# A hybrid attention layer: the products of the softmax weights with the values, for two tiles of keys at a time or for up to four

## The chip, the cores and the metric

The program runs on one core of a Trainium2 chip. The metric is the time of one execution on the device in microseconds (us); the figure for a kernel is the median of several executions.

## What is computed

One layer of a decoder with 1024 tokens and a width of 1024. Two mixers run in parallel on the same input: a gated delta rule over 8 heads, and sparse attention with 16 query heads in 4 groups of keys and values, 64 wide. After them come two gated projections and an MLP of width 4096. All is float32. The change touches the sparse attention alone, and of its three branches (compressed, selected, window) the second and third:

```
# selected: each query takes 8 blocks of 64 keys; window: each query takes the last 256 keys
s = q . k - slope * dist
p = softmax(where(mask, s, NEG))
o_slc, o_win = p_slc @ v_slc, p_win @ v_win
o = gate0 * o_cmp + gate1 * o_slc + gate2 * o_win
...
mix = sigmoid(g_dn) * (o_dn @ w_proj_dn) + sigmoid(g_ns) * (o @ w_proj_nsa)
x = x + mix @ w_out
x = x + relu(rmsnorm(x) @ w_up)^2 @ w_down
```

## The kernel before

The program has three stages. First come the projections of the input and the delta rule, then the sparse attention (about 1117 to 1589 us of the profiled span), then the output projections and the MLP.

The sparse attention is a list of 32 items: 4 groups (g) by 8 tiles of 128 queries (t). `item` (line 1113) plans one item i. Each piece of work is given a due time in units of items by `at3`; the pieces of all items are sorted by due time and written in that order (line 1369). The build then makes from it the order of the instructions of each engine, in which a piece may still be split or moved by a few places.

An item works on two branches. The selected branch (br 0) has t + 1 tiles of 128 keys, the window branch (br 1) up to three. For a tile of keys there are two pieces:

- `weights` (line 1242): TensorE writes the scores of four heads into a PSUM tile T of 128x512, by two matmuls with 512 columns (a third one, T<-cb, adds the causal mask on some tiles). ScalarE (ACT) takes the exponential into a tile P in SBUF. There are two banks for T and six buffers for P.
- `values` (line 1256): eight small products, one for each of four heads and two halves of the queries, with 64 columns of P as the stationary operand and 65 columns of the values as the moving one, summed into the PSUM tile O (in the trace o<-vv,P). O is one tile in one bank, used by all branches and items. In the order of the program such a product is one row, in the trace it is two matmuls: a tile of keys is 8 rows of the order and 16 matmuls of the trace.

After the last tile of a branch `join` (line 1264) reads O on VectorE (DVE): a reciprocal into coef, a product with the gate, a product into bs; POOL then adds bs to acc (VectorE does in the last item). After the window branch `turn_out` (line 1274) transposes acc on TensorE into a PSUM tile m, which has two banks, and `turn_store` stores it by ACT and a DMA.

Between these pieces TensorE also does the work of later items: `peak` (line 1210), scores into S (two banks) whose minimum VectorE takes; the compressed branch (tiles m); and `dn_part` (line 1336), the output projection of the delta rule, in g.

The change is in the due times of `values`. Tile j of n in an item is weighed at i + j/n. Its products are due at

```
lag = min(0.3, 2.5 / n)
j0 = j - (0 if br == 0 else t + 1)
e = i + (j + (j0 % 2 == 0 and not last)) / n + lag
```

where j0 counts the tiles within the branch: the products of an even tile are put to the time of the odd one behind it, so that they come in pairs.

Of the kernel before, what the change touches and what calls it, by code (L numbers as in the profile page):

```python
# [146 lines left out]
def body(ctx: ExitStack, tc: tile.TileContext, A, out):  # L147
# [825 lines left out]
    for h in range(NDN):  # L973
        head(h, s)
        last = s
# [117 lines left out]
    def at3(when, fn, *args):  # L1093
        if when < 0:
            when = max(1.6 * when, 1e-3 * when - 4.9)
        at(FULL + 1 + when, 0.5, fn, *args)
# [16 lines left out]
    def item(i, g, t):  # L1113
# [185 lines left out]
        for br in range(2):  # L1299
            n = spans[br][1]  # L1300
# [9 lines left out]
        n = len(tiles)  # L1310
        lag = min(0.3, 2.5 / n)
        for j, (br, k) in enumerate(tiles):
            at3(i + j / n, weights, br, k)
            first = j == 0 or tiles[j - 1][0] != br
            last = j == n - 1 or tiles[j + 1][0] != br

            j0 = j - (0 if br == 0 else t + 1)
            e = i + (j + (j0 % 2 == 0 and not last)) / n + lag
            times.append(e)
            at3(e, values, br, k, first, last)  # L1320
            if last:
                ends.append((e, join, turn_out, turn_store, br))
# [31 lines left out]
    for half in range(2):  # L1354
        at3(0.2 + 16 * half, dn_rows, half)
        for c in range(8):
            e = 1.5 + 2 * (8 * half + c)
            if half and c >= 6:
                e = 22 + 2 * c
# [5 lines left out]
    for i, (g, t) in enumerate(seq):  # L1365
        item(i, g, t)
# [382 lines left out]
```

## Time and profile before

| what | us |
|---|---|
| median of 3 runs | 2424.12 (2423.66 to 2424.78) |
| the profiled execution | 2423.24 |
| its span, first to last instruction | 2421.5 |
| TensorE (PE) busy | 2355.4 (97%) |
| VectorE (DVE) busy | 1565.8 (65%) |
| ScalarE (ACT) busy | 1092.0 (45%) |
| POOL busy | 565.7 (23%) |

PE is the time of matmuls, PEld that of the loads of their stationary operand, which can run beside matmuls. Matmuls overlap: one of 512 columns is listed with some 0.39 us, and the next starts 0.23 us after it. So the pace of TensorE is read from the starts in a timeline, not from the durations. A matmul is named by what it writes and reads, o<-vv,P for instance.

### The profile page before, as it was taken

How to read it: one execution, taken by the hardware profiler on the slowest of the kernel's cores; microseconds unless marked ns; L12 is line 12 of the kernel's file. 1: busy time of each engine (PE TensorE's matmuls, PEld its weight loads, DVE VectorE, ACT ScalarE, POOL GpSimd, SP SyncE). 2: the span in 40 equal slices, each digit the busy share in tenths (PEclk: the TensorE clock that was granted, in tenths of full speed). 3: DMA queues.
4: the chain of work that ended last, by engine and by line, in shares of the span. 5: the costliest groups of instructions: out<-in, count | busy, mean ns of one | idle time of the engine just before them, and what ended most of it. 6: DMA issues, size and time to landing. Idle time of an engine off the chain costs nothing. (4 is left out here: it accounts for less than half of the span.)

```text
span 2421.5 us, 44385 instructions
## 1 busy us (share of the span) xinstructions
PE 2355.4 (97%) x16673; PEld 1921.2 (79%) x16673; DVE 1565.8 (65%) x3626; ACT 1092.0 (45%) x2258; POOL 565.7 (23%) x473
## 2 busy tenths in 40 slices
PE   7999999999999999999999999999989999989999
PEld 5887878787878887876777777778877888878887
DVE  6666664747484848247777786643397666686785
ACT  4244343333343443227665766532256555534443
POOL 3132321203231423000010101012144444260320
PEclk9999999999999999999999999999999999999999
DMA  5421313131222221237442422164425443566343
GB/s 178 131 61 60 85 42 93 41 90 45 80 50 80 55 72 50 85 121 187 115 116 70 115 88 63 41 203 159 159 75 179 152 144 129 197 237 229 113 123 104
DMA packets 237510, 267.37 MB, mean 110 GB/s; under 512 B 76976, under 2 KB 128496, under 8 KB 237168
## 3 DMA queue, kind: packets, MB, share of 16 engines
q1 hardware_dynamic: 237296, 264.55, 35.6%
q8 instruction: 131, 2.15, 0.4%
q14 instruction: 83, 0.68, 0.1%
HBM read 190.05 MB, written 72.38 MB: 108 GB/s over the span
## 5 line engine op out<-in xcount | busy, mean ns | idle before, releaser
L177 PE MATMUL g<-hh,wh 128*128 128x512 f32 (+1 forms) x816 | 336.9, 413 | 6.7 <-ACT hh L174 6.0
L177 PE MATMUL g<-hl,wh 128*128 128x512 f32 (+1 forms) x816 | 328.6, 403 | 0.1
L177 PE MATMUL g<-hh,wl 128*128 128x512 f32 (+1 forms) x816 | 324.7, 398 | 0.1
L177 PE MATMUL V<-big,wh 128*128 128x512 f32 x768 | 238.2, 390 | 2.5 <-DVE c L1592 2.5
L186 DVE TENSOR_TENSOR wl<-a,wh 128x512 fp32r<-128x512 f32 x192 | 163.8, 855 | 111.3 <-ACT wh L174 111.3
L174 ACT ACTIVATE wh<-wr 128x512 fp32r<-128x512 f32 x210 | 131.9, 629 | 209.2 <-PE g L177 133.7
L174 ACT ACTIVATE wh<-a 128x512 fp32r<-128x512 f32 x192 | 121.0, 630 | 218.6 <-PE V L177 111.5
L1223 DVE CUSTOM_DVE_ANT_0 junk<-S,cst 128x384 f32<-128x384 f32 (+3 forms) x320 | 168.4, 532 | 66.2 <-PE S L177 62.7
L277 DVE TENSOR_TENSOR wl<-wr,wh 128x512 fp32r<-128x512 f32 x178 | 123.5, 697 | 110.7 <-ACT wh L174 109.7
L174 ACT ACTIVATE P<-T 128x512 f32<-128x512 f32 x228 | 134.6, 595 | 106.7 <-PE T L177 93.9
L177 PEld LDWEIGHTS g<-hh,wh 128*128 128x128 f32 (+1 forms) x816 | 154.4, 189 | 35.1 <-ACT hh L174 6.2
L177 PEld LDWEIGHTS g<-hh,wl 128*128 128x128 f32 (+1 forms) x816 | 154.1, 189 | 29.9 <-issue 0.6
L177 PEld LDWEIGHTS g<-hl,wh 128*128 128x128 f32 (+1 forms) x816 | 154.6, 189 | 27.2 <-DVE hl L324 1.7
L177 PEld LDWEIGHTS V<-big,wh 128*128 128x128 f32 x768 | 143.9, 188 | 33.2 <-ACT c L174 2.1
L177 PE MATMUL V<-big,wl 128*128 128x512 f32 x384 | 149.6, 390 | 3.1 <-DVE wl L186 3.1
L177 PEld LDWEIGHTS o<-vv,P 128*64 128x64 f32 x3648 | 120.3, 137 | 39.7 <-issue 27.9
L177 PE MATMUL g<-wh,hh 128*128 128x256 f32 x512 | 147.4, 288 | 0.0
L1272 POOL TENSOR_TENSOR acc<-acc,bs 128x256 f32<-128x256 f32 x62 | 48.2, 778 | 414.8 <-DVE bs L1270 292.9
L177 PE MATMUL g<-wl,hh 128*128 128x256 f32 x512 | 144.8, 283 | 0.0
L177 PE MATMUL g<-wh,hl 128*128 128x256 f32 x512 | 144.8, 283 | 0.0
L177 PE MATMUL o<-vv,P 128*64 128x65 f32 x3648 | 141.5, 226 | 0.0
L177 PE MATMUL S<-ks,qc 96*128 96x384 f32 (+3 forms) x320 | 125.5, 407 | 1.7 <-DVE mx L1223 1.2
(371 smaller groups left out, 5701.8 us busy)
## 6 DMA issues: line engine op xcount, KB each, us to landing
bb<-acd SPq DMA_DIRECT2D x112, 256.0 KB, 2.8
wr<-in_w_dn_dram SPq DMA_DIRECT2D x64, 256.0 KB, 2.8
a<-in_w_u_dram SPq DMA_DIRECT2D x64, 256.0 KB, 3.3
acd<-c SPq DMA_DIRECT2D x64, 256.0 KB, 2.8
a<-in_w_d_dram SPq DMA_DIRECT2D x64, 256.0 KB, 5.2
wr<-in_w_nb_dram SPq DMA_DIRECT2D x32, 256.0 KB, 2.7
wr<-in_w_gt_dram SPq DMA_DIRECT2D x32, 256.0 KB, 2.7
gtd<-fx SPq DMA_DIRECT2D x32, 256.0 KB, 2.2
```

What stands on the lines that cost most here:

```text
L174: return SC.activation(o, i, fn, **kw)
L177: return PE.matmul(o, l, r, start=start, stop=stop, skip_group_check=True)
L186: V.tensor_tensor(lo, src, f(hi), OP.subtract)
L277: V.tensor_tensor(wl, wr, f(wh), OP.subtract)
L1223: V.tensor_tensor_reduce(junk[:, :w], ps[:, :w], mask[:, a:b], 1.0, 3e38, OP.add, OP.min, o)
L1272: adds.tensor_tensor(acc, acc, b, OP.add)
```

## The change

The products of a branch with m tiles now come in k4 = ceil(m / 4) groups of size = ceil(m / k4) tiles, and each group is due at the time of its last tile. For m = 1 to 8 the groups are 1; 2; 3; 4; 3 and 2; 3 and 3; 4 and 3; 4 and 4.

```
-            j0 = j - (0 if br == 0 else t + 1)
-            e = i + (j + (j0 % 2 == 0 and not last)) / n + lag
+            j0, m = (j, t + 1) if br == 0 else (j - t - 1, n - t - 1)
+            k4 = -(-m // 4)
+            size = -(-m // k4)
+            e = i + (j - j0 + min(m, (j0 // size + 1) * size) - 1) / n + lag
             times.append(e)
             at3(e, values, br, k, first, last)
             if last:
                 ends.append((e, join, turn_out, turn_store, br))
```

The due times of `weights`, of the last products of a branch, of `join` and of `turn_out` are the same as before. The number of instructions of each kind is the same; only their order changes. Two places on TensorE and one on ACT show it.

TensorE, in an item with seven tiles of keys in the selected branch; T are the scores of a tile, S and m<-cst belong to later items. Before:

```order
L177 MATMUL S<-ks,qc_11318 128x128
L177 MATMUL o<-vv,P 64x65 x16
L177 MATMUL T<-qd,kd 128x512
...
L1235 MATMUL m<-cst_114,mts_11347 112x128
L177 MATMUL o<-vv,P 64x65 x16
L177 MATMUL S<-ks,qc_11318 128x128
...
L1190 MATMUL m<-cst_114,pc 128x128 x2
L177 MATMUL o<-vv,P 64x65 x8
L177 MATMUL T<-qd,kd 128x512
```

And now:

```order
L177 MATMUL S<-ks,qc_11318 128x128
L177 MATMUL o<-vv,P 64x65 x32
L177 MATMUL T<-qd,kd 128x512
...
L1235 MATMUL m<-cst_114,mts_11347 112x128
L177 MATMUL S<-ks,qc_11318 128x128
...
L1190 MATMUL m<-cst_114,pc 128x128 x2
L177 MATMUL o<-vv,P 64x65 x24
L177 MATMUL T<-qd,kd 128x512
```

Four tiles stand in the first stretch and three in the second, where three stretches stood.

TensorE, in the window branch of the same item (three tiles):

```order
 L177 MATMUL S<-ks,qc_11318 128x128
-L177 MATMUL o<-vv,P 64x65 x16
 L177 MATMUL m<-vcb,PT 128x128 x2
 L177 MATMUL T<-qd,kd 128x512
 L177 MATMUL T<-qc_11325,ks 128x512
-L177 MATMUL o<-vv,P 64x65 x8
+L177 MATMUL o<-vv,P 64x65 x24
 L177 MATMUL S<-ks,qc_11318 128x128
```

The products of the first two tiles have moved behind the scores T of the next item, into one stretch with those of the third.

ACT, some items earlier; P<-T are the exponentials, the rest prepares later items and weights:

```order
 L174 ACTIVATE P<-T 128x512
 L174 ACTIVATE wh<-wr 128x512
-L174 ACTIVATE P<-T 128x512
+L174 ACTIVATE P<-T 128x512 x2
 L174 ACTIVATE qc_11322<-qraw 64x512
-L174 ACTIVATE P<-T 128x512 x2
+L174 ACTIVATE P<-T 128x512
 L174 ACTIVATE qc_11325<-m 16x512
```

One exponential has moved ahead of a copy of a query.

## Rows read from the trace of the kernel before

**Rows 1.** The page: busy time by engine, and TensorE's clock in 40 slices.
```profile
PE 2355.4 (97%) x16673; PEld 1921.2 (79%) x16673; DVE 1565.8 (65%) x3626; ACT 1092.0 (45%) x2258; POOL 565.7 (23%) x473
...
PEclk9999999999999999999999999999999999999999
```

**Rows 2.** Busy time by stretch: window and length; PE, PEld, DVE, ACT, POOL; clock, DMA share, GB/s.
```profile
0.00:1117.00 1117.00, 1078.90 (x7883) 898.27 (x7885) 686.34 (x1649) 423.33 (x874) 255.74 (x244) 0.99 0.28 81
1117.00:1589.00 472.00, 469.86 (x5276) 361.04 (x5272) 337.72 (x1280) 297.87 (x755) 48.49 (x64) 1.00 0.32 92
1589.00:2421.00 832.00, 806.59 (x3528) 661.92 (x3524) 541.73 (x698) 370.84 (x630) 261.51 (x165) 0.99 0.48 160
```

**Rows 3.** Groups by form, 1117 to 1589 us: busy, mean ns, idle time before, its enders.
```profile
L177 PE MATMUL o<-vv,P 128*64 128x65 f32 x3648 | 141.5, 226 | 0.0
L174 ACT ACTIVATE P<-T 128x512 f32<-128x512 f32 x226 | 133.4, 595 | 106.7 <-PE T L177 93.9 <-PE S L177 10.9
L177 PEld LDWEIGHTS o<-vv,P 128*64 128x64 f32 x3644 | 120.2, 137 | 39.4 <-issue 27.5 <-DVE cmx L1148 3.1 <-DVE bs L1270 2.1
...
L1223 DVE CUSTOM_DVE_ANT_0 junk<-S,cst 128x384 f32<-128x384 f32 x174 | 94.8, 552 | 16.8 <-PE S L177 14.8
```

**Rows 4.** Timeline of PE around two stretches of o: start, time to the end, instruction, count.
```profile
1303.48 0.33 PE L177 MATMUL S<-ks,qc 96*128 96x384 f32 x1
1303.74 0.69 PE L177 MATMUL o<-vv,P 128*64 128x65 f32 x16
1304.36 0.44 PE L177 MATMUL S<-ks,qc 96*128 96x384 f32 x1
...
1306.56 0.34 PE L177 MATMUL S<-ks,qc 96*128 96x384 f32 x1
1306.83 1.15 PE L177 MATMUL o<-vv,P 128*64 128x65 f32 x32
1307.91 0.50 PE L177 MATMUL T<-qd,kd 128*128 128x512 f32 x1
1308.25 0.40 PE L177 MATMUL T<-qc,ks 128*128 128x512 f32 x1
1308.49 0.34 PE L177 MATMUL S<-ks,qc 96*128 96x384 f32 x1
1308.67 0.38 PE L1277 MATMUL m<-cst,acc 128*128 128x128 f32 x2
...
1310.51 0.40 PE L177 MATMUL T<-qd,kd 128*128 128x512 f32 x1
1310.75 0.40 PE L177 MATMUL T<-qc,ks 128*128 128x512 f32 x1
```

**Rows 5.** The same stretch on PEld, the loads of stationary operands; idle time in brackets.
```profile
1306.33 0.19 PEld L177 LDWEIGHTS S<-ks,qc 96*128 96x128 f32 x1
1306.82 1.01 PEld L177 LDWEIGHTS o<-vv,P 128*64 128x64 f32 x32 [0.31 <-issue]
1307.91 0.19 PEld L177 LDWEIGHTS T<-qd,kd 128*128 128x128 f32 x1
1308.02 0.19 PEld L177 LDWEIGHTS T<-qc,ks 128*128 128x128 f32 x1
```

**Rows 6.** Waits, 1117 to 1589 us: us in total, times, longest.
```profile
PEld o L177 <- issue: 27.5, 102, 0.4
...
PEld T L177 <- ACT P L174: 2.4, 7, 0.5
...
PEld o L177 <- DVE bs L1270: 2.1, 6, 0.4
...
PEld m L1277 <- POOL acc L1272: 1.8, 6, 0.6
...
PE m L1277 <- POOL acc L1272: 0.6, 2, 0.4
...
PEld o L177 <- ACT P L174: 0.5, 2, 0.2
```

## The prediction

> **What bounds the kernel now.** I read the page first, then the busy time by stretch, then the groups and waits of the stretch that the change touches, and last a timeline of TensorE in it. On the page TensorE is busy for 97% of the span, and its granted clock is at the upper of its two levels, 2.4 GHz, in every slice [rows 1]. By stretch, the sparse attention lasts 472 us; PE is busy for 469.9 us of it, DVE for 337.7, ACT for 297.9, and the DMA engines for a share of 0.32 [rows 2]. So in this stage TensorE sets the time and the others have room: ACT is busy for 63% of it, DVE for 72%. ACT's exponentials stand idle 93.9 us for the scores T [rows 3]: ACT waits for TensorE there, not TensorE for ACT.
>
> "Busy" hides what matters here. A matmul's time to its end overlaps the next one's, so TensorE can lose time between two kinds of matmuls without being listed as idle. The starts show it. Inside a stretch of o the loads of weights follow one another; but before one the weight unit stands idle 0.31 us, and the load starts together with the first matmul (1306.82 and 1306.83), while between two T matmuls the load is ahead of its matmul by 0.23 us (1308.02 for 1308.25) [rows 4, 5]. Over the stage the weight unit is idle 39.4 us before loads of o, 27.5 us of it 102 times with no engine to wait for [rows 3, 6]. Every stretch of o thus seems to have a fixed price at its two ends.
>
> **The price of one stretch**, from the starts in [rows 4]:
> - Inside. 32 matmuls take 1307.91 - 1306.83 = 1.08 us up to the next start, 16 take 1304.36 - 1303.74 = 0.62. Sixteen more cost 0.46, so 0.62 - 0.46 = 0.16 us is fixed.
> - In front. The S of 384 columns before a stretch holds the next start back for 1306.83 - 1306.56 = 0.27 us; the same S before another matmul takes 1308.67 - 1308.49 = 0.18. That is 0.09.
> - Behind. The first T after a stretch takes 1308.25 - 1307.91 = 0.34 us to the next start, the same T in the middle of others 1310.75 - 1310.51 = 0.24. That is 0.10.
>
> The sum is 0.35 us a stretch. For bounds: if the 0.10 behind belonged to something else, 0.25 is left; each of the readings is rounded to 0.01, and the largest sum that these allow is about 0.39. I take 0.35, since both examples show all three parts.
>
> **How many stretches go.** By the rule, pairs give sum(ceil((t+1)/2)) = 20 stretches in the selected branch of a group and 14 in the window branch, 136 in four groups; the new rule gives 12 + 8 = 20, or 80. In the orders made at the build, where a stretch may be cut by another matmul and two may touch, there are 153 unbroken stretches of o on TensorE before and 102 now, both with 1824 rows. I take the orders: 51 fewer. 51 x 0.35 = 17.9 us (12.8 to 19.9 with the bounds). The matmuls themselves, 3648 of them, stay, and so do T, S, g and m.
>
> **What the longer stretches cost.** A group of four tiles holds TensorE for 64 x 0.46 / 16 + 0.16 = 2.0 us, a pair for 1.08. Three covers have to hold:
> - P has six buffers. The products of a group still come 2.5 tiles (the lag) behind the scores of its last tile, so up to 4 + 2.5 tiles of P are alive: all six buffers are in use at n = 11. The next exponential that needs a buffer belongs to a T that stands behind the group on TensorE, so it doesn't wait for it in a circle. I cost it at nothing; if the scores ran ahead of the products, ACT would stand still with all that is queued behind it.
> - T has two banks. During a group ACT can finish two exponentials and must then wait; it goes on as soon as T follows. Now the weight unit waits 2.4 us, 7 times, for ACT's P before a T [rows 6].
> - O is one tile. The first product of a branch waits for `join` to read it, 2.1 us in all [rows 6]. The first products of the window branch now come three tiles after the end of the selected branch instead of two, and those of the next item up to four tiles in: this wait can only shrink. Against it, `turn_out` waits for POOL's sum, 1.8 + 0.6 us now [rows 6], and after a shorter stretch of TensorE's time the same chain (coef, bs, acc) has less cover.
>
> The waits that can grow are 2.4 + 1.8 + 0.6 = 4.8 us. The mean stretch grows by 153/102 = 1.5; I let the waits grow in the same ratio, by 2.4 us. Bounds: nothing, and a doubling, 4.8 us.
>
> The few moves on ACT, DVE and SP's queue are of one or two places; each engine's work is the same, and these three have idle time in the stage. The DMA engines are busy for a third of it [rows 2], so a load that goes out a few places later is still early. The two other stages hold the same instructions in the same order and move in time as a whole.
>
> **The sum.** -17.9 + 2.4 = -15.5 us. The profiled execution took 2423.2 us, its span is 2421.5, and the median of the runs is 2424.1; a difference within one stage carries over to each alike, so I forecast 2424.1 - 15.5 = **2408.6 us**. Ends: 19.9 gained and nothing given back, 2404.2; 12.8 gained and 4.8 given back, 2416.1.
>
> **A rule that speaks against it.** The rows have the load of o's first weights start with its matmul, 0.31 us after the weight unit fell idle [rows 5]. The Trainium skill, page "TensorE: Matmul & The Clock Gate", section "Architectural detail: the array is 16× 32×32, not 1× 128×128", says that TensorE's queue can pull loads of weights ahead of matmuls in flight. By that alone the ends of a stretch would be hidden and cutting their number would bring nothing; it is the third rival below. The same skill's page "TensorEngine Tiling (Array Packing)", section "Key Properties", says that changing the tiling mode drains TensorE, without a figure. The trace agrees with the first rule between T and T (0.23 us ahead) and with the second one before o.
>
> **The rivals.**
> 1. *VectorE's S takes the gain in part.* S has two banks, and its minimum takes 0.55 us on DVE [rows 3]. If S matmuls bunch behind the longer stretches, the third waits. Some 54 stretches of the new order hold about three tiles or more; a wait of 0.17 us (what is left of 0.55 after a pair of T at 0.23 each, rounded up) at each is 9 us: 2424.1 - 17.9 + 9 = 2415 us. For it: DVE is the second busiest. Against: it is idle 28% of the stage, and S and T still alternate in the order.
> 2. *TensorE waits for the newest P* (the slower side). If the exponential of a group's last tile is not done when TensorE comes to the group, each of the 54 long stretches waits up to one exponential, 0.595 us [rows 3]: 54 x 0.595 = 32 us, 2424.1 - 17.9 + 32 = 2438 us. The point from which it decides is an ACT that runs more than the lag of 2.5 tiles behind. Against it: the lag of the last tile is as before, and o waited for P twice, 0.5 us in all [rows 6].
> 3. *The price isn't one of a stretch.* If what I read as fixed ends is work that only moves (TensorE idles at the same places for other reasons), nothing changes: 2424 us. Against it: the S in front of each of the two stretches is held back alike (0.27 and 0.26 us), and no engine ends most of that idle time of PEld.
>
> **How the numbers follow.** Forecast 0.76, first rival 0.12, third rival 0.07, second rival 0.05. The first two are faster by over 0.2% (4.8 us, about what a measurement of this kernel can tell from no change): 0.88; within it 0.07; slower 0.05. The range from 2404 to 2417 us holds the forecast with its bounds and the first rival; the other two, 0.12, are left out.
>
> **What would show it.** Right: the stage shrinks from 472 to some 456 us with the same matmuls; the idle time of PEld before o falls from 39.4 us to about 39.4 x 102/153 = 26; the time from a stretch's first start to the next start is 0.16 + 0.029 per matmul also at 64 matmuls (2.0 us); the waits of T for P and of m for acc grow by a few us at most. Wrong: a stretch of 64 takes more than twice one of 32, or the waits of PE for P, for S's minimum or for acc grow by more than 10 us together, or the clock in the stage leaves the upper level.

## The result and the profile after

The changed kernel takes 2408.51 us (2402.47 to 2410.13, 4 runs) beside 2423.89 us (2422.20 to 2424.78, 4 runs) for the kernel before on the same chip: a ratio of 0.9933 with a 95% interval of 0.9918 to 0.9948, that is 12.6 to 19.9 us less. The forecast was 2408.6 us. In a second comparison (e9 below) it took 2408.52 us beside 2424.21, a ratio of 0.9935 (0.9922 to 0.9947).

The profiled execution has a span of 2407.3 us instead of 2421.5. The work is the same. TensorE's busy time fell by 15.6 us; that of DVE, ACT and POOL moved by 3.3 us at most. This is the page's first part, the same line as in [rows 1]:

```profile
PE 2339.8 (97%) x16673; PEld 1916.8 (80%) x16673; DVE 1563.8 (65%) x3626; ACT 1093.4 (45%) x2258; POOL 569.0 (24%) x473
```

Where the time went is read from the first and the last o. The view of the instructions that write or read the tile O gives both; first the row of the kernel before, then that of the changed one (times of one in ns, then the first and last start in us):

```profile
L177 PE MATMUL o<-vv,P x3648: 222/222/272, 1116.8 to 1588.9; 128*64 128x65 f32 x192
```

```profile
L177 PE MATMUL o<-vv,P x3648: 222/222/272, 1113.7 to 1573.3; 128*64 128x65 f32 x192
```

The stage between them took 472.1 us and takes 459.6: 12.5 us less. It begins 3.1 us earlier, though nothing was changed ahead of it, and what follows it takes 1.4 us more (2407.3 - 1573.3 = 834.0 instead of 832.6). That the earlier begin isn't the change's doing is seen in a stretch far ahead of it. Busy time between 20 and 100 us, kernel before and changed kernel, columns as in [rows 2]:

```profile
20.00:100.00 80.00, 71.35 (x352) 55.55 (x353) 57.40 (x103) 19.94 (x43) 16.61 (x18) 0.94 0.44 123
```

```profile
20.00:100.00 80.00, 70.72 (x363) 55.28 (x363) 58.67 (x104) 20.17 (x43) 16.61 (x18) 0.98 0.44 129
```

The instructions are the same there, but the granted clock was 0.94 in one execution and 0.98 in the other. At 100 us the changed kernel is already 2.2 us ahead by the same matmul. That share differs from one execution to the next, so the length of the stage is the better measure of the change, and it is given below for every kernel.

Inside the stage the rows answer to [rows 3] (groups by form, changed kernel, 1117 to 1575 us, so 28 matmuls at the stage's begin lie outside):

```profile
L177 PE MATMUL o<-vv,P 128*64 128x65 f32 x3620 | 129.1, 225 | 0.0
...
L177 PEld LDWEIGHTS o<-vv,P 128*64 128x64 f32 x3616 | 114.9, 138 | 26.6 <-issue 20.2 <-DVE wl L277 1.1 <-DVE bs L1270 1.1
```

The idle time of the weight unit before loads of o fell from 39.4 us to 26.6; 39.4 x 102/153 is 26.3. And the price of a stretch is the same for longer ones, as the starts show (timeline of PE, changed kernel, as [rows 4]):

```profile
1300.76 0.40 PE L177 MATMUL g<-oh,wl 128*128 128x512 f32 x1
1301.08 1.62 PE L177 MATMUL o<-vv,P 128*64 128x65 f32 x48
1302.63 0.50 PE L177 MATMUL S<-ks,qc 96*128 96x512 f32 x1
1302.97 0.40 PE L177 MATMUL T<-qd,kd 128*128 128x512 f32 x1
1303.21 0.40 PE L177 MATMUL T<-qc,ks 128*128 128x512 f32 x1
1303.44 0.39 PE L177 MATMUL S<-ks,qc 96*128 96x512 f32 x1
1303.67 0.39 PE L177 MATMUL T<-qd,kd 128*128 128x512 f32 x1
...
1318.76 2.09 PE L177 MATMUL o<-vv,P 128*64 128x65 f32 x64
1320.78 0.50 PE L177 MATMUL T<-qd,kd 128*128 128x512 f32 x1
1321.12 0.40 PE L177 MATMUL T<-qc,ks 128*128 128x512 f32 x1
```

Forty-eight matmuls take 1.55 us to the next start and 64 take 2.02, after 0.62 for 16 and 1.08 for 32: again 0.46 to 0.47 for each 16 and 0.16 over. The trace has twelve stretches of 64, and each takes 2.02 us. Before the stretch of 48 g is held back (0.32 us to the next start instead of 0.23), behind it S (0.34 instead of 0.23, the row at 1303.44).

What was given back stands in the waits (changed kernel, 1117 to 1575 us, as [rows 6]):

```profile
PEld m L1277 <- POOL acc L1272: 4.9, 13, 0.8
PEld T L177 <- ACT P L174: 4.9, 13, 0.6
...
PE m L1277 <- POOL acc L1272: 1.2, 5, 0.3
PEld o L177 <- DVE bs L1270: 1.1, 3, 0.4
PE T L177 <- ACT P L174: 0.8, 3, 0.4
```

The transposes m wait 6.1 us for POOL's acc, after 2.4 before; T waits 5.7 us for P, after 2.6 (of which 0.2 on PE itself, in a row that [rows 6] leaves out). Together 6.8 us more. In a second profile of the same kernel (e9 below) m waits 6.0 us, but T only 3.4, together 4.4 us more. From the first to the last o, S waits for its minimum 2.7 and 2.9 us in the two profiles, after 1.9.

The rows that name bs for o, 2.1 us before and 1.1 now, are no such wait. They are 6 and 3 times some 0.35 us, which is what the weight unit stands idle before a stretch in any case: in the kernel before, the last T in front of o is followed by it after 0.32 or 0.33 us in three of the four places between T and o where bs is named, and after 0.32 to 0.33 where no engine is.

Why m waits can be counted in the traces. From the first step of `join` behind an item's window branch to the transposes, TensorE had 21 matmuls of o before, on the mean of the 32 items, and has 4 now; in half of the items they were 32 before, or 1.08 us. They are the next item's first products, which now come behind the transposes, and POOL's sum is no faster than before.

### The profile page after: what moved, and what is told of

Same layout as the page of the kernel before. It is cut to its first block, busy times and chain, and to the rows that moved or that the text cites. A ratio compares the mean times of both kernels' runs of the same rounds, so it can differ in the third digit from the quotient of the medians.

```text
span 2407.3 us, 44378 instructions
## 1 busy us (share of the span) xinstructions
PE 2339.8 (97%) x16673; PEld 1916.8 (80%) x16673; DVE 1563.8 (65%) x3626; ACT 1093.4 (45%) x2258; POOL 569.0 (24%) x473
## 5 line engine op out<-in xcount | busy, mean ns | idle before, releaser
L177 PE MATMUL o<-vv,P 128*64 128x65 f32 x3648 | 130.1, 225 | 0.0
```

The source lines that it names most:

```text
L177: return PE.matmul(o, l, r, start=start, stop=stop, skip_group_check=True)
```

## The experiments

The theory (A) is that of the prediction: each unbroken stretch of o costs a fixed time at its ends, because TensorE goes from matmuls with 128 stationary columns to some with 64 and back; the time goes with the number of stretches. The rivals are that the place of the products matters and not the number of stretches (B), and that the price is one of the type, float32 products between matmuls of another type (C).

Stage means first to last start of o. The kernels e1 to e4 are compared with one set of runs of the kernel before (median 2423.37 us), e5 to e8 with a second (2423.26), e9 to e12 with a third (2424.21), each set on the chip of its four kernels.

| kernel | stretches | time, us | ratio to before (95%) | stage, us |
|---|---|---|---|---|
| before | 153 | | | 472.1 |
| the change | 102 | 2408.51 | 0.9933 (0.9918 to 0.9948) | 459.6 |
| e1, cut by 128 columns | 161 | 2425.48 | 1.0010 (0.9999 to 1.0021) | 472.9 |
| e2, cut by 64 columns | 161 | 2412.08 | 0.9952 (0.9937 to 0.9968) | 461.2 |
| e3, o with 128 columns | 101 | 2474.28 | 1.0204 (1.0180 to 1.0227) | 521.9 |
| e4, no groups | 219 | 2442.85 | 1.0078 (1.0061 to 1.0095) | 492.3 |
| e5, selected branch alone | 123 | 2417.16 | 0.9978 (0.9968 to 0.9987) | 465.7 |
| e6, window branch alone | 133 | 2415.27 | 0.9968 (0.9958 to 0.9979) | 464.4 |
| e7, late transposes | 100 | 2405.20 | 0.9924 (0.9910 to 0.9938) | 454.5 |
| e8, e7 and copies on POOL | 100 | 2409.97 | 0.9948 (0.9933 to 0.9962) | 455.9 |
| e9, the change again | 102 | 2408.52 | 0.9935 (0.9922 to 0.9947) | 458.4 |
| e10, e7 again | 100 | 2405.21 | 0.9926 (0.9913 to 0.9938) | 455.2 |
| e11, e7 with lag 2.2 / n | 91 | 2408.03 | 0.9934 (0.9922 to 0.9945) | 456.9 |
| e12, e7 with lag 2.4 / n | 92 | 2407.76 | 0.9932 (0.9919 to 0.9944) | 456.5 |

**e1 and e2: cut the long stretches where they stand.** One small matmul stands between the second and the third tile of a group; its result goes into a column of O that nobody reads. e1 takes 128 stationary columns for it, e2 takes 64.

```
-        def values(br, k, first, last):
+        def values(br, k, first, last, cut):
...
+            if cut:
+                mm(O[0:128, 0, 80:81], identb[:, 0:128], identb[:, 0:1], False, False)
...
-            at3(e, values, br, k, first, last)
+            cut = j0 % size == 1 and (j0 + 1) % size and j0 + 1 < m
+            at3(e, values, br, k, first, last, cut)
```

> The change, with one small bf16 matmul (128 stationary columns, 1 moving column, into an unused column of O) between the second and the third tile of each group of three or four: 60 of them, which cut the 102 stretches of o into 161; nothing else moves. If a stretch has a fixed price because TensorE goes from 128 stationary columns to 64 and back (theory A), each cut costs 0.35 us and the small matmul 0.03: 60 x 0.38 = 23 us, 2431 us, and the gain of the change is gone although the products stand where the change put them. If the gain came from the place of the products and not from the number of stretches (theory B), only the small matmuls are paid, 60 x 0.03 to 0.1 us: 2410 to 2415 us.

> As e1, with 64 stationary columns in place of 128 in the small bf16 matmul. If the price is that of the number of stationary columns (theory A), nothing but the small matmul is paid, 60 x 0.03 to 0.06 us: 2410 to 2413 us. If it is one of the type, float32 products between matmuls of another type (theory C), it costs what e1 costs, 2431 us.

Measured: 2425.48 and 2412.08 us. Sixty small matmuls that differ only in their stationary columns make 13.4 us, or 11.7 in the stage, 0.22 or 0.20 us each. A stretch of 32 with its cut, timeline of PE in e1:

```profile
1311.72 1.15 PE L177 MATMUL o<-vv,P 128*64 128x65 f32 x32
1312.81 0.18 PE L177 MATMUL o<-cb 128*128 128x1 bf16 x1
1312.91 0.69 PE L177 MATMUL o<-vv,P 128*64 128x65 f32 x16
1313.53 0.50 PE L177 MATMUL S<-ks,qc 96*128 96x512 f32 x1
```

and in e2:

```profile
1301.10 1.15 PE L177 MATMUL o<-vv,P 128*64 128x65 f32 x32
1302.08 0.17 PE L177 MATMUL o<-cb 128*64 128x1 bf16 x1
1302.09 0.68 PE L177 MATMUL o<-vv,P 128*64 128x65 f32 x16
1302.69 0.45 PE L177 MATMUL S<-ks,qc 96*128 96x384 f32 x1
```

From the first o to the o behind the cut it is 1.19 us in e1 and 0.99 in e2: 0.20 us for leaving and entering the width of 64. To the start behind the whole stretch it is 1.81 and 1.59 us, where an uncut stretch of 48 takes 1.55: with the same width a matmul of another type in between costs 0.04 us. The loads of the two small matmuls are listed with 0.10 us in e1 and 0.11 in e2 (timeline of PEld), so the difference isn't that of a longer load. B falls (the products of e1 stand where the change put them, and the gain is gone), and C falls for this part. But e1 was expected at 2431 with 0.35 us a cut: the third part of the price, 0.10 us behind a stretch, isn't paid at a cut, since o follows and not T or S.

The Trainium skill, page "TensorEngine Tiling (Array Packing)", section "Key Properties", says that changing the tiling mode drains TensorE. The two runs agree, with 0.20 us for a change there and back.

**e3: o with the width of all others.** Four products with 128 stationary columns for a tile instead of eight with 64.

```
-                for q in Q2:
-                    mm(O[q, 2 * (r % 2) + r // 2, 0:65], P[:, r, q], vv[:, k, br, 0:65], first and r == 0, last)
+                mm(O[:, 2 * (r % 2) + r // 2, 0:65], P[:, r, :], vv[:, k, br, 0:65], first and r == 0, last)
```

> The change, with o computed by four products of 128 stationary columns for a tile (both halves of the queries at once) in place of eight of 64. The pace of 128 x 128 float32 matmuls is 0.11 us in the trace (m<-vcb), so a tile takes 8 x 0.11 = 0.9 us instead of 0.46: 228 x 0.43 = +98 us. Theory A: the ends of the stretches cost nothing any more, 102 x 0.35 = -36 us: 2471 us, and the S or T in front of o is not held back (0.18 and 0.24 us instead of 0.27 and 0.33). Theory C (price of the type): the ends stay, 2507 us.

Measured: 2474.28 us, 65.8 over the change, where A gave some 62; the stage is 62.3 us longer. Timeline of PE:

```profile
1309.98 1.90 PE L177 MATMUL o<-vv,P 128*128 128x65 f32 x16
1311.71 0.39 PE L1190 MATMUL m<-cst,pc 128*128 128x128 f32 x2
...
1315.90 0.34 PE L177 MATMUL S<-ks,qc 96*128 96x384 f32 x1
1316.08 2.79 PE L177 MATMUL o<-vv,P 128*128 128x65 f32 x24
1318.68 0.42 PE L177 MATMUL S<-ks,qc 96*128 96x384 f32 x1
1318.94 0.40 PE L177 MATMUL T<-qd,kd 128*128 128x512 f32 x1
```

S in front of o takes its 0.18 us, nothing is held back. Sixteen matmuls take 1.73 us and 24 take 2.60, 0.108 each both times, with nothing over. But the S behind o still takes 0.26 us instead of 0.18. The kernel before shows the same without o:

```profile
1302.47 0.71 PE L177 MATMUL m<-vcb,PT 128*128 128x128 f32 x4
1302.93 0.47 PE L177 MATMUL T<-qd,kd 128*128 128x512 f32 x1
1303.25 0.39 PE L177 MATMUL T<-qc,ks 128*128 128x512 f32 x1
```

These m have 128 stationary columns, and T behind them takes 0.32 us to the next start, not 0.24. Like o they are of the type float32 in the kernel, while T, S and g are of the type float32r (the rows of matmuls list both as f32). So of the three parts of the price the first two (0.16 inside, 0.09 in front) belong to the width, and 0.08 of the third stands behind float32 products of any width; why it does isn't shown. The narrow form is right all the same: 0.46 us a tile against 0.87.

**e4: no groups.** Each tile's products by themselves, at `e = i + j / n + lag`; `join` is due at e + 0.05 instead of e + 0.08.

> No grouping: the products of each tile by themselves, 219 stretches against 153 before and 102 with the change (join is due 0.03 of an item earlier, so that it stands before the next products). Theory A: 66 x 0.35 = 23 us over the kernel before, less some 3 us of waits: 2444 us. Theory B: no law in the number; the products come earlier than in the kernel before, so waits for P may grow, but 2424 us within 5.

Measured: 2442.85 us; the stage is 20.2 us longer than before for 66 more stretches, 0.31 each. The rows name bs before loads of o with 8.4 us here after 2.1, but most of that is the price of the stretches under another name: of the eight places where bs is named between T<-qd,kd and o, the starts are 0.32 to 0.33 us apart in six, as where no engine is named, and 0.51 and 0.62 in two.

**e5 and e6: one branch at a time.** The new size in the selected branch alone (`size = -(-m // k4) if br == 0 else 2`) or in the window branch alone.

> The new groups in the selected branch alone, pairs in the window branch: 123 stretches of o, 30 fewer than before. Theory A, with the net price of 0.28 us a stretch that the stages of the kernels so far give (117 stretches between 102 and 219 make 32.7 us): 30 x 0.28 = 8.4 us, 2415 us beside a kernel before of 2423.5. If only long groups of four paid (or only short ones), it would be nearer to either end, 2409 or 2423 us.

> The new groups in the window branch alone, pairs in the selected one: 133 stretches, 20 fewer than before. Theory A: 20 x 0.28 = 5.6 us, 2418 us beside a kernel before of 2423.5; together with e5 the gains make up that of the change (50 of 51 stretches).

Measured: 2417.16 and 2415.27 us. In the stage e5 gains 6.4 us with 30 stretches (0.21 each) and e6 gains 7.7 with 20 (0.39 each). The net price isn't the same in both branches, against the expectation, and the waits say why: m waits for acc 6.1 us in e5 (2.4 before) and 2.2 in e6; T waits for P 3.4 and 1.9 us (2.6 before). So the wait of m comes with the groups of the selected branch: between `join` and the transposes TensorE has 4 matmuls of o on the mean in e5, as with the change, and 21 in e6, as before. With these waits given back, e5 has (6.4 + 3.7 + 0.8) / 30 = 0.36 us a stretch, and e6 (7.7 - 0.2 - 0.7) / 20 = 0.34.

**e7 and e10: take the new wait away.** The change, with the transposes of acc and their store later, so that POOL's sum is made when TensorE comes to them.

```
-                at3(e + 0.3, turn_out)
-                at3(e + 0.4, turn_store)
+                at3(e + 0.5, turn_out)
+                at3(e + 0.6, turn_store)
```

> The change, with turn_out and turn_store of the window branch due 0.2 of an item later, so that TensorE comes to the transposes of acc when POOL has long made it: 100 stretches. If the waits of m for acc that grew with the change (2.4 us before, 6.1 us after) are time lost, they go: 4 to 6 us under the change, 2403 to 2405 us. If TensorE would wait for something else at that place, it stays at 2408 us.

> e7 again on the same chip as e9: 3 to 5 us under it (m waits for acc 6.1 us with the change, 0.7 us in e7). If the difference between e7 and the change was one of chips, none is left.

Measured: 2405.20 and 2405.21 us, 3.3 us under the change both times, and the stage is 454.5 and 455.2 us. The waits in e7 (1110 to 1590 us):

```profile
PEld S L177 <- DVE mx L1223: 3.1, 10, 0.6
PEld T L177 <- ACT P L174: 2.9, 9, 0.4
...
PEld m L1277 <- POOL acc L1272: 0.7, 2, 0.5
```

The wait of m is 0.9 us (0.2 of it on PE, in a row not shown) after 6.1, and the stage is shorter by 459.6 - 454.5 = 5.1 us, and by 3.2 from e9 to e10; by 0.35 us each, the two stretches fewer make 0.7 of it. So at least a good part of the wait was lost time, though the 95% intervals of e7 and e10 still overlap with those of the change. This version has the lowest time of all here.

**e8: less work for ACT.** e7, and the copies wh of the delta rule's output weights are made by POOL instead of ACT.

> As e7, and the copies of the delta rule's output weights (32 of 128x512, 0.63 us each on ACT) are made by POOL in the sparse stage. If T waits for P (5.7 us after the change) because ACT is held by such copies, the waits fall to some 3 us, and it is 2 to 3 us under e7: 2401 to 2402 us. If ACT's load doesn't matter there, it stays with e7; if POOL's copies hold up the sums for acc, m waits for acc again and it is some us slower than e7.

Measured: 2409.97 us, worse than e7, and not in the way that was expected. T waits for P 2.6 us, hardly less than in e7. But from the first to the last o S waits for its minimum on DVE 6.7 us, after 3.0 in e7 and e10. In e8 (groups by form, 1123 to 1580 us) a copy takes 775 ns on POOL, and DVE's next step wl stands still for it:

```profile
L276 POOL CAST wh<-wr 128x512 fp32r<-128x512 f32 x29 | 22.5, 775 | 89.0 <-PE g L177 76.0 <-DMA wr<-in_w_pd_dram 12.6 <-PE T L177 0.3
L277 DVE TENSOR_TENSOR wl<-wr,wh 128x512 fp32r<-128x512 f32 x30 | 22.3, 750 | 6.5 <-POOL wh L276 6.4
```

DVE waits 6.4 us for POOL there (in e10 1.8 us for ACT's copies), but only one of S's waits, of 0.31 us, has a wl in the 2.5 us before it. The longest one, 1.09 us on PEld and 0.66 on PE at 1143.3 us, stands behind these steps of DVE:

```profile
1139.30 1.61 DVE L186 TENSOR_TENSOR ol<-ra,oh 128x1024 fp32r<-128x1024 f32 x1 [0.66 <-ACT oh L174]
1140.84 0.58 DVE L1169 TENSOR_TENSOR im<-im,cst 128x16 f32<-128x16 f32 x1
```

In e10 they take 1.22 and 0.19 us on the mean. Both ran beside POOL's copies here (POOL has three between 1139.2 and 1142.6 us). So DVE's steps beside the copies are the likelier cause of S's waits, though no run tests it. Of the 4.8 us between e8 and e7 the stage has only 1.4. The profile of e8 begins its stage late (first o at 1123.1 us), 10.4 us behind e7: 3.4 us of it are there before 1080 us, and 5.5 come between 1085 and 1096 us, where DVE waits 6.9 us for a load of constants (cst), as it does in e1, and TensorE stands still behind it. What of the difference between the medians this explains wasn't settled.

**e9: the change again.**

> The change again, beside e10 to e12 on the same chip: 2408.5 us as before, and the stage from the first to the last o near 459.6 us. If the stage's length is the same to 1 us while the time of the whole moves by several us, what moves lies in the stages that the change doesn't touch.

Measured: 2408.52 us, the stage 458.4 us, 1.2 off the first profile. The profiled execution of e9 took 2413.4 us with a stage that is shorter than in the one of 2409.1: what moves a run by some us lies outside the stage.

**e11 and e12: still fewer stretches.** In the items with few tiles the build cuts groups, since their lag of 0.3 is less than 2.5 tiles. A lag of 2.2 / n or 2.4 / n for all n leaves 91 or 92 stretches.

```
-        lag = min(0.3, 2.5 / n)
+        lag = 2.2 / n
```

> e7 with lag = 2.2 / n for all n in place of min(0.3, 2.5 / n): in the items with few tiles the products come later, fewer stretches are cut, and 91 are left instead of 100. Theory A: 9 x 0.3 = 2.7 us under e10. If with the shorter lag of the long items o waits for the newest P (0.5 us before), it is slower instead, up to 0.6 us for each of some 20 groups, 10 us.

> e11 with lag = 2.4 / n: 92 stretches, 2.4 us under e10, and the waits for the newest P nearer to those of the change.

Measured: 2408.03 and 2407.76 us, 2.8 and 2.6 us over e10 where 2.7 and 2.4 less were expected; the stage is 1.7 and 1.3 us longer than in e10. The intervals overlap with that of e10, so what is shown is that eight or nine stretches fewer didn't pay, not that they cost something. o doesn't wait for the newest P. Waits in e11 (1110 to 1590 us):

```profile
PEld S L177 <- DVE mx L1223: 7.5, 25, 0.8
PEld T L177 <- ACT P L174: 4.9, 11, 0.9
...
PE S L177 <- DVE mx L1223: 0.9, 3, 0.4
...
PE T L177 <- ACT P L174: 0.7, 2, 0.5
```

S waits for DVE 8.4 us after 3.6 in e10, and T for P 5.6 after 3.1: 7.3 us of new waits against some 3 us of price, more than the stage lost. This is the prediction's first rival, S on VectorE, at a point where it takes the gain.

## Why the prediction was right, and where it was off

- **The bound.** TensorE sets the stage, and "busy" hides its losses: right. Its listed busy time fell with no matmul taken away. The granted clock was 1.00 in the stage in both profiles, so the clock has no part in it.
- **The price of a stretch, 0.35 us.** Right in size: 12.5 us of the stage and 6.8 us of grown waits of T and m make 19.3 us for 51 stretches, 0.38 each; the second profile gives (13.7 + 4.4) / 51 = 0.35, e5 and e6 0.36 and 0.34, and e4 (20.2 + 1.5) / 66 = 0.33, its T and m waiting 1.5 us less than before. The waits of S would add up to 0.04. Its parts have two causes: some 0.20 to 0.25 goes with the change of width (e1 against e2, e3), 0.08 stands behind float32 products of any width (e3, and m in the kernel before). The upper bound of 0.39 was too low for what it says: the rounding of all the starts in the sum allows 0.42.
- **The count, 51 from the orders and not 56 from the rule.** The trace has 153 and 102 stretches, as the orders.
- **The waits, 2.4 us.** This term was mis-sized: I let the waits of 4.8 us grow with the mean stretch, by half, with a doubling, 4.8 us more, as the bound. They grew by 6.8 us in one profile, past that bound, and by 4.4 in the other. What was wrong is the ratio: the cover of acc didn't shrink with the mean stretch, but lost the next item's first products as a whole (21 matmuls of o on the mean before, 4 now), while the chain of join and POOL is as long as before. e7 took this wait away, and its time is 3.3 us less.
- **P's six buffers, O and the lag.** The longer groups cost nothing there: o waits for P 0.5 us as before. The 2.1 us that the prediction reads as o's wait for `join` were six times the price of a stretch, with bs as the name of its end; of the four with T in front, one start is 0.18 us later than where no engine is named.
- **The sum.** The stage gained 12.5 and 13.7 us in two profiles where 15.5 was forecast. That the median agrees with the forecast to 0.1 us is in part luck: 2 to 3 us of it lie outside the stage or in the spread of the runs, whose interval is 12.6 to 19.9 us. Both comparisons of medians have 15.4 and 15.7 us; why they have more than the stage isn't settled.
- **The rivals.** Rival 3 (no price of a stretch) is ruled out by e1 and e2. Rival 2 (waits for the newest P) did not occur in any run. Rival 1 (S on DVE) came to about 1 us with the change (2.7 and 2.9 us after 1.9), but took the gain of e11 and e12. Its 0.17 us for a stretch doesn't follow from its own terms: 0.55 less twice 0.23 leaves 0.09, which would be 4.9 us and a time of 2411.

## What to carry to other kernels

Matmuls with a narrow stationary operand are worth it inside a stretch (0.46 us a tile here against 0.87), but each change of width and back has a price that no busy time shows; put them side by side and read the price from the starts of the neighbours. Count stretches in the order that the build makes, and after merging them look at what now comes too early behind them: here a transpose due at a fixed distance, and moving it was worth a fifth as much again. Past that point fewer stretches brought nothing more here, since the waits of other engines grew.

## What was not expected of the hardware

- A matmul with one moving column between two stretches of the same width costs 0.04 us in all (1.59 us in e2 for a stretch of 48 with it, 1.55 without), though its type is another; with 128 stationary columns it makes the pair of starts 0.20 us longer.
- Two products with 64 stationary columns side by side take 4 matmuls of the trace, 0.116 us; the one with 128 that replaces them takes 2, 0.216 us.
- Equal instructions take unequal time from one execution to the next at the start of the program: the granted clock between 20 and 100 us was 0.98, 0.94 and 0.91 in three profiles (the change, before, e8). By 100 us the change was 2.2 us ahead of the kernel before, so a difference of 2 us between two spans of this kernel can come from there alone.
